# Preparing the tokens of the first projection in blocks of 416 after the first one, with the sums of squares on VectorE, the copies of K on ScalarE and part of the first weights loaded by GpSimd

## The chip, the cores and the metric

The kernel runs on one core of a Trainium2 chip. Its engines are TensorE (PE in the profile), VectorE (DVE), ScalarE (ACT) and GpSimd (POOL); SyncE (SP) issues DMAs, and so do the queues of ScalarE and GpSimd. Each engine takes its instructions in one fixed order and waits on semaphores. The metric is the device time of one execution in microseconds; the number given for a kernel is the median of its runs.

## The reference

One layer of a streaming encoder, for 2048 prompt tokens and 32 sample tokens. The part that the change touches is the beginning:

```
shift_m, scale_m, ... = split(silu(c) @ w_ada + b_ada)        # per sequence: prompt, sample
h = rmsnorm(x, g_pre_mix) * (1.0 + scale_m) + shift_m         # x: (tokens, 1024)
z = h @ w_in                                                  # (1024, 5136), all mixers' inputs
```

where rmsnorm multiplies x by 1 / sqrt(mean of squares + 1e-6). From z come a banded attention, a gated linear attention, their merge and output projection, and then a gated MLP with a causal convolution. All of that follows unchanged.

## The kernel before

**Layout.** Tokens are columns: x is read as xT, 8 slices k of 128 channels by 2080 tokens (2048 prompt, then 32 sample). Matmuls work on pairs: a number is split into a rounded hi part and the remainder lo, and mm3 (L74) makes three matmuls per product, hi with hi (L78), hi with lo (L79), lo with hi (L80). The normed tokens h are kept as two tiles of hi and lo, hA for the first four blocks of NB = 416 tokens and hB for the fifth.

**The first stage.** Here the kernel computes the adaLN vectors, norms all tokens, and already projects them on 512 columns of w_in, Q and K of the gated linear attention, in a "wave" (L341): for each block of 416 tokens, for each k, for four chunks of 128 output columns, three matmuls, all into four PSUM tiles (tag px, six buffers). So a block takes 96 matmuls of 416 columns. A wave ends with four evacuations (t_evac, L202): Q by ScalarE with a factor (L230), K by VectorE (L233), each into a tile tx (two buffers) that is stored by a DMA of ScalarE's queue (L235).

**The norm by half blocks** of NH = 208 tokens, ten of them, numbered hb. prep_load (L263) loads two tiles of four k each (tag xk, six buffers). prep_stats (L270) squares them on ScalarE (L276, L279), two k at a time, and adds them up: on VectorE for hb 0 and 1, on GpSimd for the others (L280, L281). rstd_bcast (L140) splits the sum (sh on ScalarE, sl on VectorE), and its finish multiplies it by a matrix of ones on TensorE, so that the sum over channels stands in every partition (pst, L148 and L149, a PSUM tile of the same tag px); then ScalarE takes Ln and Exp (L154, L155) and VectorE corrects with three operations (L156 to L158): the reciprocal root. prep_apply (L290) then makes, for each k, x times scale times root on VectorE (L299), the hi part with the shift on ScalarE (L300) and the lo part on VectorE (L301). For hb 2 and odd k GpSimd does the scaling (L288, L297). The last half block has its 176 prompt and 32 sample tokens apart, since their scale and shift differ.

**The adaLN vectors** scale and shift come in four pieces each: ada_load (L305) brings 1 MB in two DMAs, ada (L314) multiplies with packed matmuls (L320), the result is turned by four small matmuls (L327), and mod_finish adds bias and gain. Piece j gives channels k = 2j and 2j + 1, so the norm of block 0 proceeds two k at a time as pieces arrive.

**The weights** of the wave, two of 256 columns, are loaded in four pieces of two k each (w_pieces, L180; L187 is the DMA on SP, two buffers wr for both weights) and split (L191 ScalarE, L192 VectorE).

**What sets the order.** TensorE's order is the order in which the code is written (a manual schedule). The other engines' and queues' orders come from a scheduler that simulates the kernel ahead of time and prefers, among what is ready, what is written earlier. Written by hand is thus where in TensorE's stream the ones matmul of a half block stands: for hb 4 and later after the first k of each half of a wave (L434 to L436). Block 0 (L353 to L418) is written out with the adaLN pieces, the weights' pieces and hb 2 and 3 between its k. The blocks 1 to 4 follow in a loop over half blocks (L422). Then come the other columns of w_in in tiles of tokens (L564), with the later adaLN vectors on the side.

Of the kernel before, what the change touches and what calls it, by code (L numbers as in the profile page):

```python
# [20 lines left out]
KD = 8  # L21
# [9 lines left out]
NB = 416  # L31
# [27 lines left out]
def encoder_step(ctx: ExitStack, tc: tile.TileContext, I, O):  # L59
# [30 lines left out]
    onef = consts.tile([128, 128], F32, name="onef")  # L90
    nc.vector.memset(onef, 1.0)
    ones = consts.tile([128, 128], F32R, name="ones")
    nc.vector.tensor_copy(ones, onef)
# [46 lines left out]
    def rstd_bcast(pl, pps, tag, s, n, w, bufs=1):  # L140
# [5 lines left out]
        def finish():  # L146
# [6 lines left out]
            r = pl.tile([128, w], F32, name="rstd", tag="rstd", bufs=bufs)  # L153
# [4 lines left out]
            nc.vector.scalar_tensor_tensor(r[:, :n], t[:, :n], 1.5, r0[:, :n], op0=OP.add, op1=OP.mult)  # L158
            return r[:, :n]
# [20 lines left out]
    def w_pieces(wp, c0, n, w, kp, wr=2):  # L180
# [4 lines left out]
        def piece(kk):  # L185
            raw = wp.tile([128, kp, w], F32, name="wr", tag="wr", bufs=wr)
            d = nc.sync.dma_start(raw[:, :, :n], dap(w_in, kk * 128 * WIN + c0, [[WIN, 128], [128 * WIN, kp], [1, n]]))  # L187
# [14 lines left out]
    def t_evac(stg, kind, c, b, p):  # L202
# [22 lines left out]
        if kind == "g":  # L225

            nc.scalar.activation(x, p, AF.Tanh, scale=0.5)
            dst = sgT
        elif kind == "Q":
            nc.scalar.activation(x, p, AF.Copy, scale=0.125)  # L230
            dst = qbT
        else:
            nc.vector.tensor_copy(x, p)  # L233
            dst = kbT
# [8 lines left out]
    with ExitStack() as st:  # L243
# [8 lines left out]
        scp = pp.tile([128, KD, 32], F32, name="scp")  # L252
# [7 lines left out]
        XK = {}  # L260
        POOL = {2: (1, 3, 5, 7)}

        def prep_load(hb, q_=nc.sync):  # L263
            XK[hb] = []
            for k in range(0, KD, 4):
                x = pp.tile([128, 4, NH], F32, name="xk", tag="xk", bufs=6)
                q_.dma_start(x, dap(I["xT"], k * 128 * T + NH * hb, [[T, 128], [128 * T, 4], [1, NH]]))
                XK[hb].append(x)

        def prep_stats(hb, add):  # L270

            sq = pp.tile([128, 2, NH], F32, name="sq", tag="sq", bufs=2)
            for k in range(0, KD, 2):
                x = XK[hb][k // 4][:, k % 4:k % 4 + 2]
# [3 lines left out]
                s2 = pp.tile([128, 2, NH], F32, name="sq2", tag="sq2")  # L278
                nc.scalar.activation(s2, x, AF.Square)  # L279
                add.tensor_add(sq, sq, s2)  # L280
            add.tensor_add(sq[:, 0], sq[:, 0], sq[:, 1])  # L281
            return lambda: rstd_bcast(pp, psx, "px", sq[:, 0], NH, NH, 2)

        def prep_scale(hb):
            for k in POOL.get(hb, ()):
                for a, e, s in parts(NH * hb, NH):
                    xs = XK[hb][k // 4][:, k % 4, a:e]
                    nc.gpsimd.tensor_scalar(xs, xs, mod[:, 1, k, s:s + 1], 1.0, op0=OP.mult, op1=OP.mult)  # L288

        def prep_apply(hb, r, ks_=range(KD)):  # L290
            for k in ks_:
                for a, e, s in parts(NH * hb, NH):
                    hi, lo = [h_at(x, k, NH * hb + a, e - a) for x in range(2)]
                    xs = XK[hb][k // 4][:, k % 4, a:e]
                    s1, s2 = mod[:, 1, k, s:s + 1], mod[:, 0, k, s:s + 1]
                    if k in POOL.get(hb, ()):
                        nc.gpsimd.tensor_mul(xs, xs, r[:, a:e])  # L297
                    else:
                        nc.vector.scalar_tensor_tensor(xs, xs, s1, r[:, a:e], op0=OP.mult, op1=OP.mult)  # L299
                    nc.scalar.activation(hi, xs, AF.Identity, bias=s2)  # L300
                    nc.vector.scalar_tensor_tensor(lo, xs, s2, f32(hi), op0=OP.add, op1=OP.subtract)  # L301

# [11 lines left out]
        def ada(j, v):  # L314
# [7 lines left out]
            r = pp.tile([128, 256], F32, name="mr", tag="mr")  # L322
# [12 lines left out]
        prep_load(0)  # L335
        prep_load(1)
        ada_load(0, 0)
        first = [("Q", 1536), ("K", 1792)]
        w0, steps = zip(*[w_pieces(wp, c0, 256, 272, 2, 2) for _, c0 in first])
# [13 lines left out]
        fin0 = prep_stats(0, nc.vector)()  # L353
# [25 lines left out]
        for s_ in steps:  # L379
            s_[2]()  # L380
# [1956 lines left out]
```

## Time and profile before

| | us |
|---|---|
| median of 3 runs | 3160.36 |
| lowest and highest run | 3156.84, 3162.19 |
| the profiled execution | 3162.02 |
| its span, from first to last instruction | 3160.3 |
| first wave matmul (block 0) | 27.21 |
| first matmul after the last wave (block 4) | 163.85 |

The profile shows one execution. A row of the groups names the line, engine, operation, the tile written and those read, the shape, the count, the busy time, the mean duration in ns, and then the idle time of the engine just ahead of such instructions with what ended it. A row of the waits names who waited for whom: us in total, times, the longest. A row of the stretches gives for each engine the busy time and number of instructions, then the TensorE clock granted (1.00 is full), the DMA engines' busy share and GB/s. In the order of time a row begins with the start and the time it took; x4 means four instructions in a row. Durations of one instruction include time in which the next has already begun.

### The profile page before, as it was taken

What the parts mean: (1) busy time and instruction counts of PE and PEld (TensorE: products, weight loads), DVE (VectorE), ACT (ScalarE), POOL (GpSimd) and SP (SyncE); (2) the same over time, 40 slices, a digit from 0 to 9 for tenths busy, and PEclk for the clock granted to TensorE, in tenths of its full rate; (3) what the DMA queues carried; (4) which work ended last, traced back from release to release, by engine and by line L of the source; (5) the groups of instructions that cost most, each with busy time, mean ns of one, the idle gap of its engine ahead of it and who ended that gap; (6) DMA issues with size and microseconds to landing.
All of it is one profiled execution on the core that took longest, in us unless ns stands there. A gap on an engine that the chain in (4) does not pass through costs nothing. (4 is left out here: it accounts for less than half of the span.)

```text
span 3160.3 us, 56426 instructions
## 1 busy us (share of the span) xinstructions
PE 3047.7 (96%) x19748; PEld 2947.7 (93%) x19748; DVE 2239.8 (71%) x4879; ACT 1648.8 (52%) x3792; POOL 269.4 (9%) x427
## 2 busy tenths in 40 slices
PE   6999999999999999999999999999999999999997
PEld 4899999998999999988999899999999999999997
DVE  6735617774555555566677799998888778897877
ACT  4522224443555555544454655567666556576755
POOL 2201201112111111120000000000000000000001
PEclk9999999999999999999999999999999999999998
DMA  7354435554433334575457686788897667888784
GB/s 220 91 156 125 139 98 142 137 137 128 130 109 111 107 100 117 169 230 184 140 175 227 211 256 210 223 256 225 249 265 217 189 189 230 263 250 284 242 267 146
DMA packets 598478, 580.12 MB, mean 184 GB/s; under 512 B 53201, under 2 KB 526530, under 8 KB 598194
## 3 DMA queue, kind: packets, MB, share of 16 engines
q1 hardware_dynamic: 553026, 527.86, 56.2%
q10 hardware_dynamic: 44432, 47.34, 4.7%
q8 instruction: 155, 2.54, 0.3%
q0 software_dynamic: 736, 1.33, 0.2%
q14 instruction: 129, 1.06, 0.1%
HBM read 388.71 MB, written 187.65 MB: 182 GB/s over the span
## 5 line engine op out<-in xcount | busy, mean ns | idle before, releaser
L1882 PE MATMUL ad<-hA,hB 128*128 128x350 f32 (+2 forms) x1734 | 301.7, 324 | 3.8 <-DVE hB L1824 2.4
L1882 PEld LDWEIGHTS ad<-hA,hB 128*128 128x128 f32 x1734 | 282.5, 189 | 5.5 <-DVE hB L1824 3.3
L78 PE MATMUL pm<-hA,wh 128*128 128x416 f32 x768 | 287.4, 374 | 0.0
L79 PE MATMUL pm<-hA,wh 128*128 128x416 f32 x768 | 269.3, 351 | 0.0
L80 PE MATMUL pm<-hA,wl 128*128 128x416 f32 x768 | 269.3, 351 | 0.0
L1824 DVE TENSOR_TENSOR hA<-raws,hA 128x512 fp32r<-128x512 f32 (+1 forms) x367 | 241.9, 668 | 13.0 <-ACT hA L1819 12.7
L1819 ACT ACTIVATE hA<-raws 128x512 fp32r<-128x512 f32 (+1 forms) x367 | 222.0, 617 | 29.9 <-DMA raws<-in_w_up_dram 11.1
L1882 PE MATMUL ad<-hA,hA 128*128 128x348 f32 (+2 forms) x1308 | 225.5, 323 | 2.5 <-ACT work L2008 1.8
L1882 PE MATMUL g<-hA,hB 128*128 128x348 f32 (+2 forms) x1248 | 217.1, 323 | 6.4 <-ACT work L2004 3.5
L1882 PEld LDWEIGHTS ad<-hA,hA 128*128 128x128 f32 x1308 | 211.8, 188 | 3.9 <-ACT work L2008 2.4
L1882 PEld LDWEIGHTS g<-hA,hB 128*128 128x128 f32 x1248 | 202.3, 188 | 9.1 <-ACT work L2004 4.7
L1882 PE MATMUL ad<-hA 128*128 128x350 f32 (+2 forms) x1173 | 205.1, 324 | 4.2 <-DVE hA L1734 4.1
L1882 PEld LDWEIGHTS ad<-hA 128*128 128x128 f32 x1173 | 191.7, 190 | 5.0 <-DVE hA L1734 4.4
L1824 DVE TENSOR_TENSOR hB<-raws,hB 128x512 fp32r<-128x512 f32 (+1 forms) x289 | 190.9, 668 | 6.5 <-ACT hB L1819 6.1
L1819 ACT ACTIVATE hB<-raws 128x512 fp32r<-128x512 f32 (+1 forms) x289 | 175.8, 617 | 25.3 <-DMA raws<-in_w_up_dram 11.8
L69 ACT ACTIVATE pth<-pp 128x256 fp32r<-128x256 f32 (+1 forms) x288 | 106.4, 373 | 139.2 <-PE pp L1027 135.9
L72 DVE TENSOR_TENSOR ptl<-pp,pth 128x256 fp32r<-128x256 f32 (+1 forms) x288 | 118.1, 414 | 85.2 <-ACT pth L69 82.4
L78 PE MATMUL pn<-wh,hA 128*128 128x256 f32 (+1 forms) x624 | 176.9, 283 | 0.0
L79 PE MATMUL pn<-wl,hA 128*128 128x256 f32 (+1 forms) x624 | 176.3, 283 | 0.0
L80 PE MATMUL pn<-wh,hA 128*128 128x256 f32 (+1 forms) x624 | 176.1, 282 | 0.0
L1991 ACT COPY g<-ad 128x348 f32<-128x348 f32 (+2 forms) x102 | 44.3, 434 | 244.1 <-PE ad L1882 156.4
L1882 PE MATMUL g<-hA,hA 128*128 128x350 f32 (+2 forms) x894 | 157.4, 325 | 4.0 <-ACT g L1991 2.3
(507 smaller groups left out, 8468.6 us busy)
## 6 DMA issues: line engine op xcount, KB each, us to landing
raws<-in_w_up_dram SPq DMA_DIRECT2D x220, 256.0 KB, 4.3
raws<-sW SPq DMA_DIRECT2D x176, 256.0 KB, 3.8
sW<-raws SPq DMA_DIRECT2D x88, 256.0 KB, 3.6
raws<-in_w_down_dram SPq DMA_DIRECT2D x80, 256.0 KB, 5.2
wr<-in_w_in_dram SPq DMA_DIRECT2D x76, 256.0 KB, 3.2
sgT<-tx ACTq DMA_DIRECT2D x80, 208.0 KB, 1.9
wa<-in_w_ada_dram SPq DMA_DIRECT2D x64, 256.0 KB, 3.0
keys<-ks SPq DMA_DIRECT2D x128, 128.0 KB, 2.9
```

Source lines behind the costliest of these rows:

```text
L69: i = nc.scalar.activation(hi, src, AF.Copy)
L72: nc.vector.tensor_sub(lo, src, f32(hi))
L78: nc.tensor.matmul(out, ah, bh, start=first and i == 0, stop=False)
L79: nc.tensor.matmul(out, ah, bl, start=False, stop=False)
L80: nc.tensor.matmul(out, al, bh, start=False, stop=last and i == n - 1)
L1819: act = nc.scalar.activation(hi[:, :n], raw(i, n), AF.Copy)
L1824: nc.vector.tensor_sub(lo[:, :n], raw(i, n), f32(hi[:, :n]))
L1882: nc.tensor.matmul(out[:, :w], l_[:, k], r_[:, k, :w], start=first and k == 0 and i == 0, stop=k == n - 1 and i == 2, skip_group_check=True)
L1991: nc.scalar.copy(g[:, 0, :w], ad[:, 0, :w])
```

## The change

- After block 0 the norm goes by whole blocks of 416 tokens. Token tiles hold two k of a block (still six buffers); block 0 is loaded and normed in two halves as before.
- All sums of squares are VectorE's, of two k of 416 tokens at a time; GpSimd's sums and scalings go. The tiles sq, sq2, rstd have one buffer each, of the larger size.
- The ones matmul writes a PSUM tile of another pool (psm, tag pm) that is otherwise used later; px is left to the waves and the adaLN pieces.
- In blocks 1 to 3 the ones matmul of the next block stands behind six of the eight k of the wave, followed in the text by the next block's scaling and the load of the block after it. For block 1 it stands behind the sixth k of block 0.
- K is copied out of PSUM by ScalarE (t_evac's last branch).
- Of the two first weights the third and fourth piece (k from 4) are issued by GpSimd's queue (late=nc.gpsimd).
- Small tiles move: scp to another pool, mr into a tile of tag nx, the ones are made from ident in one operation.

```diff
     nc.vector.memset(eps, EPS)
-    onef = consts.tile([128, 128], F32, name="onef")
-    nc.vector.memset(onef, 1.0)
     ones = consts.tile([128, 128], F32R, name="ones")
-    nc.vector.tensor_copy(ones, onef)
+    nc.vector.tensor_scalar(ones, ident, 0.0, 1.0, op0=OP.mult, op1=OP.add)
+    onef = f32(ones)
...
-    def rstd_bcast(pl, pps, tag, s, n, w, bufs=1):
+    def rstd_bcast(pl, pps, tag, s, n, w, r=None):
...
             t = pl.tile([128, w], F32, name="rstt", tag="sl")
-            r = pl.tile([128, w], F32, name="rstd", tag="rstd", bufs=bufs)
             nc.scalar.activation(r0[:, :n], p[:, :n], AF.Ln, bias=eps, scale=1.0 / D)
...
             nc.vector.scalar_tensor_tensor(t[:, :n], t[:, :n], -0.5 / D, r0[:, :n], op0=OP.mult, op1=OP.mult)
-            nc.vector.scalar_tensor_tensor(r[:, :n], t[:, :n], 1.5, r0[:, :n], op0=OP.add, op1=OP.mult)
-            return r[:, :n]
+            nc.vector.scalar_tensor_tensor(r, t[:, :n], 1.5, r0[:, :n], op0=OP.add, op1=OP.mult)
+            return r
...
-    def w_pieces(wp, c0, n, w, kp, wr=2):
+    def w_pieces(wp, c0, n, w, kp, wr=2, late=nc.sync):
...
             raw = wp.tile([128, kp, w], F32, name="wr", tag="wr", bufs=wr)
-            d = nc.sync.dma_start(raw[:, :, :n], dap(w_in, kk * 128 * WIN + c0, [[WIN, 128], [128 * WIN, kp], [1, n]]))
+            d = (nc.sync if kk < KD // 2 else late).dma_start(raw[:, :, :n], dap(w_in, kk * 128 * WIN + c0, [[WIN, 128], [128 * WIN, kp], [1, n]]))
             if behind.pop():
...
         else:
-            nc.vector.tensor_copy(x, p)
+            nc.scalar.copy(x, p)
             dst = kbT
...
-        scp = pp.tile([128, KD, 32], F32, name="scp")
+        scp = pa.tile([128, KD, 32], F32, name="scp")
         nc.vector.memset(scp, 0.0)
...
-        XK = {}
-        POOL = {2: (1, 3, 5, 7)}
-        def prep_load(hb, q_=nc.sync):
-            XK[hb] = []
-            for k in range(0, KD, 4):
-                x = pp.tile([128, 4, NH], F32, name="xk", tag="xk", bufs=6)
-                q_.dma_start(x, dap(I["xT"], k * 128 * T + NH * hb, [[T, 128], [128 * T, 4], [1, NH]]))
-                XK[hb].append(x)
-        def prep_stats(hb, add):
-            sq = pp.tile([128, 2, NH], F32, name="sq", tag="sq", bufs=2)
+        XK, RT = {}, {}
+        def prep_load(b, ks_=range(0, KD, 2), a=0, n=NB):
+            for k in ks_:
+                if (b, k) not in XK:
+                    XK[b, k] = pp.tile([128, 2, NB], F32, name="xk", tag="xk", bufs=6)
+                nc.sync.dma_start(XK[b, k][:, :, a:a + n],
+                                  dap(I["xT"], k * 128 * T + NB * b + a, [[T, 128], [128 * T, 2], [1, n]]))
+        def prep_stats(b, a=0, n=NB):
+            sq = pp.tile([128, 2, NB], F32, name="sq", tag="sq")[:, :, :n]
             for k in range(0, KD, 2):
-                x = XK[hb][k // 4][:, k % 4:k % 4 + 2]
+                x = XK[b, k][:, :, a:a + n]
                 if k == 0:
...
                     continue
-                s2 = pp.tile([128, 2, NH], F32, name="sq2", tag="sq2")
+                s2 = pp.tile([128, 2, NB], F32, name="sq2", tag="sq2")[:, :, :n]
                 nc.scalar.activation(s2, x, AF.Square)
-                add.tensor_add(sq, sq, s2)
-            add.tensor_add(sq[:, 0], sq[:, 0], sq[:, 1])
-            return lambda: rstd_bcast(pp, psx, "px", sq[:, 0], NH, NH, 2)
-        def prep_scale(hb):
-            for k in POOL.get(hb, ()):
-                for a, e, s in parts(NH * hb, NH):
-                    xs = XK[hb][k // 4][:, k % 4, a:e]
-                    nc.gpsimd.tensor_scalar(xs, xs, mod[:, 1, k, s:s + 1], 1.0, op0=OP.mult, op1=OP.mult)
-        def prep_apply(hb, r, ks_=range(KD)):
+                nc.vector.tensor_add(sq, sq, s2)
+            nc.vector.tensor_add(sq[:, 0], sq[:, 0], sq[:, 1])
+            if a == 0:
+                RT[b] = pp.tile([128, NB], F32, name="rstd", tag="rstd")
+            return rstd_bcast(pp, psm, "pm", sq[:, 0], n, NB, RT[b][:, a:a + n])
+        def prep_apply(b, r, ks_=range(KD), a=0, n=NB):
             for k in ks_:
-                for a, e, s in parts(NH * hb, NH):
-                    hi, lo = [h_at(x, k, NH * hb + a, e - a) for x in range(2)]
-                    xs = XK[hb][k // 4][:, k % 4, a:e]
+                for c, e, s in parts(NB * b + a, n):
+                    hi, lo = [h_at(x, k, NB * b + a + c, e - c) for x in range(2)]
+                    xs = XK[b, k - k % 2][:, k % 2, a + c:a + e]
                     s1, s2 = mod[:, 1, k, s:s + 1], mod[:, 0, k, s:s + 1]
-                    if k in POOL.get(hb, ()):
-                        nc.gpsimd.tensor_mul(xs, xs, r[:, a:e])
-                    else:
-                        nc.vector.scalar_tensor_tensor(xs, xs, s1, r[:, a:e], op0=OP.mult, op1=OP.mult)
+                    nc.vector.scalar_tensor_tensor(xs, xs, s1, r[:, c:e], op0=OP.mult, op1=OP.mult)
                     nc.scalar.activation(hi, xs, AF.Identity, bias=s2)
                     nc.vector.scalar_tensor_tensor(lo, xs, s2, f32(hi), op0=OP.add, op1=OP.subtract)
+        def apply0(ks_):
+            prep_apply(0, r0, ks_, 0, NH)
+            prep_apply(0, r1, ks_, NH, NH)
...
                                  start=k < 4, stop=k >= 4)
-            r = pp.tile([128, 256], F32, name="mr", tag="mr")
+            r = stg.tile([128, 272], F32, name="mr", tag="nx")[:, :256]
             nc.vector.tensor_copy(r, p[:, :256])
...
         ada_load(0, 1)
-        prep_load(0)
-        prep_load(1)
+        prep_load(0, a=0, n=NH)
+        prep_load(0, a=NH, n=NH)
         ada_load(0, 0)
         first = [("Q", 1536), ("K", 1792)]
-        w0, steps = zip(*[w_pieces(wp, c0, 256, 272, 2, 2) for _, c0 in first])
+        w0, steps = zip(*[w_pieces(wp, c0, 256, 272, 2, 2, nc.gpsimd) for _, c0 in first])
...
-        fin0 = prep_stats(0, nc.vector)()
+        fin0 = prep_stats(0, 0, NH)
         ada_load(1, 1)
...
         r0 = fin0()
-        fin1 = prep_stats(1, nc.vector)()
+        fin1 = prep_stats(0, NH, NH)
         m1 = ada(0, 0)
...
         ps = wave_tiles()
-        fins = {}
         for s_ in steps:
...
         ada_load(2, 1)
-        prep_load(2)
         m0 = ada(1, 1)
...
         ada_load(3, 1)
-        prep_load(3)
-        prep_apply(0, r0, [0, 1])
-        prep_apply(1, r1, [0, 1])
+        apply0([0, 1])
         for s_ in steps:
             s_[2]()
+        prep_load(1, (0, 2))
         ada_load(3, 0)
-        fins[2] = prep_stats(2, nc.gpsimd)
         wave(0, (0, ), ps)
...
         m0 = ada(2, 1)
-        prep_apply(0, r0, [2, 3])
-        prep_apply(1, r1, [2, 3])
-        prep_load(4)
+        apply0([2, 3])
         for s_ in steps:
             s_[3]()
+        prep_load(1, (4, 6))
         wave(0, (1, ), ps)
...
         m1 = ada(2, 0)
-        fins[3] = prep_stats(3, nc.gpsimd)
+        fin = prep_stats(1)
         wave(0, (2, ), ps)
...
         m0 = ada(3, 1)
-        prep_apply(0, r0, [4, 5])
-        prep_apply(1, r1, [4, 5])
+        apply0([4, 5])
         wave(0, (3, ), ps)
         m0()
-        prep_scale(2)
         m1 = ada(3, 0)
-        r2 = fins.pop(2)()()
         wave(0, (4, ), ps)
         m1()
-        prep_apply(0, r0, [6, 7])
-        prep_apply(1, r1, [6, 7])
-        prep_apply(2, r2)
-        prep_load(5)
+        apply0([6, 7])
         wave(0, (5, ), ps)
-        f3 = fins.pop(3)()
-        wave(0, (6, ), ps)
-        r3 = f3()
-        wave(0, (7, ), ps)
-        prep_apply(3, r3)
-        fins[4] = prep_stats(4, nc.gpsimd)
+        r = fin()
+        prep_apply(1, r)
+        prep_load(2)
+        wave(0, (6, 7), ps)
         wave_evac(0, ps)
...
         hB.extend(arena2.tile([128, KD, NB], F32R, name=f"hB{x}") for x in range(2))
-        for s_ in range(2, 10):
-            b = s_ // 2
-            if s_ + 4 < 10:
-                prep_load(s_ + 4)
-            if s_ + 3 < 10:
-                fins[s_ + 3] = prep_stats(s_ + 3, nc.gpsimd)
-            k0 = 4 * (s_ % 2)
-            if s_ + 2 < 10:
-                fin = fins.pop(s_ + 2)()
-            if s_ % 2 == 0:
-                ps = wave_tiles()
-            if b < 4:
-                wave(b, range(k0, k0 + 1), ps)
-                prep_apply(s_ + 2, fin())
-                wave(b, range(k0 + 1, k0 + 4), ps)
-            elif s_ % 2 == 0:
-                wave(b, range(KD), ps, (0, 1))
-                wn = load_w(wp, 2048, 256, 272, 2, 2)
-            else:
-                wave(b, range(KD), ps, (2, 3))
-            if s_ % 2:
-                wave_evac(b, ps)
+        for b in range(1, 4):
+            ps = wave_tiles()
+            fin = prep_stats(b + 1)
+            wave(b, range(6), ps)
+            prep_apply(b + 1, fin())
+            if b < 3:
+                prep_load(b + 2)
+            wave(b, (6, 7), ps)
+            wave_evac(b, ps)
+        ps = wave_tiles()
+        wave(4, range(KD), ps, (0, 1))
+        wn = load_w(wp, 2048, 256, 272, 2, 2)
+        wave(4, range(KD), ps, (2, 3))
+        wave_evac(4, ps)
         prep.close()
```

## The prediction

> **What bounds the kernel now.** I read the page first, then the busy time by stretches, then who waited for whom inside the stretches that stand out, and last the order of time at one block boundary.
>
> ```profile
> span 3160.3 us, 56426 instructions
> PE 3047.7 (96%) x19748; PEld 2947.7 (93%) x19748; DVE 2239.8 (71%) x4879; ACT 1648.8 (52%) x3792; POOL 269.4 (9%) x427
> ```
>
> TensorE is busy for 96% of the span: 112.6 us in all is idle. The change lies in the stage up to the first projection's end, 164 us of 3160. So the question is how much of TensorE's idle time and slow clock lies there, and how much of that the change can reach. Whatever TensorE gains there is carried to the end, since all that follows is bound by it. Five token blocks of 416 columns go through the wave of Q and K; the stretches below are the start and then block 0, 1, 2, 3 and 4, cut where TensorE starts each of them.
>
> ```profile
> core 0: us, PE busy (x) PEld busy (x) DVE busy (x) ACT busy (x) POOL busy (x), PEclk, DMA share, GB/s
> 0.00:27.21 27.21, 12.63 (x81) 6.07 (x81) 13.10 (x40) 11.75 (x24) 0.70 (x6) 1.00 0.85 258
> 27.21:71.25 44.04, 33.29 (x186) 27.09 (x186) 31.05 (x67) 20.24 (x47) 17.31 (x20) 0.88 0.70 214
> 71.25:97.36 26.11, 22.71 (x101) 21.15 (x101) 20.61 (x46) 14.75 (x36) 13.29 (x11) 0.80 0.31 90
> 97.36:121.72 24.36, 20.00 (x102) 18.07 (x101) 18.50 (x43) 13.19 (x33) 8.01 (x9) 1.00 0.37 108
> 121.72:145.75 24.03, 21.22 (x102) 19.72 (x101) 19.16 (x57) 11.93 (x32) 2.16 (x4) 0.93 0.12 37
> 145.75:163.85 18.10, 18.10 (x97) 17.96 (x97) 13.63 (x36) 6.03 (x15) 0.00 (x0) 1.00 0.63 205
> ```
>
> Block 4, which has no later block to prepare, takes 18.10 us: 96 matmuls with nothing between them, 0.188 us each. Blocks 1, 2 and 3 do the same matmuls in 26.11, 24.36 and 24.03 us, together 74.50, though VectorE, ScalarE and GpSimd are far from full. So a chain of waits sets their length. 74.50 - 3 x 18.10 = 20.2 us is the most that the waits and the slow clock of these three can give back.
>
> ```profile
> PE px L78 <- ACT tx L230: 4.1, 4, 1.6
> PE pst L149 <- DVE sl L72: 2.3, 2, 1.7
> PE px L78 <- ACT hA L300: 2.1, 1, 2.1
> PE px L79 <- DVE hA L301: 2.1, 3, 0.8
> PE pst L148 <- ACT sh L69: 2.0, 1, 2.0
> ```
>
> These are TensorE's waits in blocks 1 to 3: for the copy out of a PSUM tile (4.1 us), for the normed tokens (hA, 4.2) and for the sum of squares (4.3), 12.6 us. The boundary from block 1 to 2, TensorE and then ScalarE:
>
> ```profile
> 97.36 0.42 PE L78 MATMUL px<-hA,wh 128*128 128x416 f32 x1
> 102.42 0.46 PE L78 MATMUL px<-hA,wh 128*128 128x416 f32 x1 [1.61 <-ACT tx L230]
> 103.32 0.37 PE L148 MATMUL pst<-sh,ones 128*128 128x208 f32 x1
> ...
> 100.78 1.18 ACT L300 ACTIVATE hA<-xk,mod 128x208 fp32r<-128x208 f32 x3 [0.86 <-DVE xk L299]
> 101.87 0.49 ACT L230 ACTIVATE tx<-px 128x416 f32<-128x416 f32 x1
> ```
>
> Twelve matmuls of the first k take 5.96 us (97.36 to 103.32) in place of 2.25. The second copy of Q stands in ScalarE's order behind the hi parts of the half block in preparation, and its PSUM tile is needed by the fourth chunk.
>
> **The sums and the size of the pieces.** Prices of the operations, one row each:
>
> ```profile
> L299 DVE SCALAR_TENSOR_TENSOR xk<-xk,mod,rstd 128x208 f32<-128x208 f32 x68 | 35.0, 558 | 0.4
> L280 POOL TENSOR_TENSOR sq<-sq,sq 128x416 f32<-128x416 f32 x24 | 29.9, 1246 | 40.0 <-ACT sq L279 39.8
> L301 DVE SCALAR_TENSOR_TENSOR hA<-xk,mod,hA 128x208 fp32r<-128x208 f32 x64 | 28.8, 497 | 1.9 <-ACT hA L300 1.9
> L279 ACT ACTIVATE sq<-xk 128x416 f32<-128x416 f32 x30 | 16.3, 544 | 17.4 <-POOL sq L280 11.9 <-DMA xk<-in_xT_dram 3.8 <-DVE sq L280 1.7
> L233 DVE COPY tx<-px 128x416 f32<-128x416 f32 x10 | 5.8, 584 | 6.5 <-DMA qbT<-tx 3.9 <-ACT rst L154 2.0 <-DMA wa<-in_w_ada_dram 0.6
> L230 ACT ACTIVATE tx<-px 128x416 f32<-128x416 f32 x10 | 4.9, 501 | 5.2 <-PE px L80 5.2
> L280 DVE TENSOR_TENSOR sq<-sq,sq 128x416 f32<-128x416 f32 x6 | 3.6, 593 | 4.5 <-ACT sq L279 4.5
> L299 DVE SCALAR_TENSOR_TENSOR xk<-xk,mod,rstd 128x176 f32<-128x176 f32 x8 | 3.2, 397 | 0.0
> L299 DVE SCALAR_TENSOR_TENSOR xk<-xk,mod,rstd 128x32 f32<-128x32 f32 x8 | 2.0, 246 | 0.0
> ...
> 73.40 1.46 DVE L299 SCALAR_TENSOR_TENSOR xk<-xk,mod,rstd 128x208 f32<-128x208 f32 x4
> ```
>
> The forms of 176 and 32 columns give VectorE's slope, (397 - 246) / 144 = 1.05 ns a column. One of 208 columns alone is then 0.397 + 32 x 1.05 ns = 0.43 us. Four undisturbed ones take 1.46 us: (1.46 - 0.43) / 3 = 0.343 us from one to the next. An operation of 416 columns then comes every 0.343 + 208 x 1.05 ns = 0.56 us. The means of 558 and 497 ns for the same 208 columns show what GpSimd's additions beside them cost: over the 64 to 68 operations, (558 + 497 - 2 x 430) x 66 = 13 us of VectorE.
>
> VectorE for one block, without disturbance. Before: 32 operations x 0.343 = 11.0, two chains of three for the reciprocal root at 0.43 each 2.6, two splits 0.7, two K copies 1.2, together 15.5. After: 16 x 0.56 = 9.0, one chain 3 x 0.65 = 2.0, one split 0.6, and new the sums of squares: three of 832 columns (593 ns + 416 x 1.05 = 1.03) and one of 416, 3.7; the K copies gone: 15.3. So VectorE takes over GpSimd's sums for nothing, since half the operations of the rest disappear, and GpSimd's disturbance goes. 15.3 fits under TensorE's 18.1. Block 4 has its last 32 columns by themselves, as before, and its preparation costs 2 us more, under the same cover.
>
> ScalarE per block: four squares of 832 columns at most 1.09 (twice 544), eight hi parts of 416 at about 0.55 (between the copy's 501 and the square's 544 ns), Ln, Exp and the split the same, 1.6, four copies 2.0 of which two (K) are new, four DMA issues 1.5: some 14 us of 18 (the issues by an estimate from SP's 0.37). It has room, so the K copies cost nothing themselves. But they add a wait in its queue, taken up below.
>
> **The chain across a boundary, after.** The matmul with the ones now stands behind six of the eight k of a block (T). In the trace it and the first scaling of the next tokens stand thus:
>
> ```profile
> 138.78 0.26 PE L148 MATMUL pst<-sh,ones 128*128 128x208 f32 x1
> ...
> 141.36 1.04 DVE L299 SCALAR_TENSOR_TENSOR xk<-xk,mod,rstd 128x176 f32<-128x176 f32 x4
> ```
>
> 2.58 us for 208 columns; with 416, the two matmuls grow by 0.1 each (0.188 us for 416 above), Ln and Exp by some 0.17 each (an estimate beneath VectorE's slope), three VectorE operations by 0.22 each: T + 3.8. VectorE in this trace does up to four scalings in a row (73.40 above); if they stand ahead of the first lo part, the first lo is ready at T + 3.8 + 4 x 0.56 + 0.65 = T + 6.7. TensorE has the two ones matmuls (0.4) and 24 matmuls (4.5) to do, to T + 4.9. It waits 1.8 us, and I add 0.2 for the copies: 2.0 per boundary in place of 5.96 - 2.25 = 3.7. From there TensorE takes 2.25 us per k and VectorE gives one every 1.12, so it doesn't wait again.
>
> Then the next T. The second half of the next tokens can be loaded only when the first half of this block's buffers is read out (six buffers of two k, four per block), at about T + 9. A load takes this long:
>
> ```profile
> 88.16 0.37 SPq L267 DMA_DIRECT2D xk<-in_xT_dram  x1
> ...
> 91.62 0.55 ACT L276 ACTIVATE sq<-xk 128x416 f32<-128x416 f32 x1 [1.58 <-DMA xk<-in_xT_dram]
> ...
> qbT<-tx ACTq DMA_DIRECT2D x10, 208.0 KB, 2.7
> ks<-ql POOLq DMA_DIRECT2D x10, 104.0 KB, 2.7
> ```
>
> 3.5 us from issue to use. T + 12.5; two squares and two sums in turn (the buffer for squares is single) 4.2, the last sum 0.6, the split 1.2: T + 18.5. TensorE reaches the next ones matmul at T + 4.9 + 2.0 + 13.5 = T + 20.4. 1.9 us of slack; I charge 0.5 for orders that don't fit. The block: 18.1 + 0.4 + 2.0 + 0.5 = 21.0, three of them 63.0 for 74.5: **-11.5 us**. Beneath, with no wait at all, 18.5; above, see the rivals.
>
> The clock: block 1 has 0.80 and 22.71 us of PE for what takes 20.00 in block 2, 2.7 us, with waits of 2.1 and 2.0 us in it; block 2 kept 1.00 with waits of 1.6 and 1.7. New waits of 2.0 lie between, nearer to the first by size but shorter in sum; I take 0 and keep 2.7 per block for the range. The Trainium skill's "TensorE: Matmul & The Clock Gate" (Part 1) puts the loss of clock at an idle window of about 3.4 us; by that the waits forecast here cost only themselves, and block 1 of this trace, whose waits are all shorter, speaks against taking it as a bound.
>
> **Block 0.** It keeps its half blocks, its adaLN pieces and its order. What changes: GpSimd's sums and scalings beside it go (17.31 us of its time here), the sums of block 1 come to VectorE (3.6), four VectorE scalings that GpSimd did come back in the larger form, and the third and fourth quarter of both weights are issued by GpSimd.
>
> ```profile
> L192 DVE TENSOR_TENSOR wl<-wr,wh 128x512 fp32r<-128x512 f32 x24 | 17.3, 723 | 19.0 <-ACT wh L191 18.7
> ...
> 50.20 1.55 DVE L192 TENSOR_TENSOR wl<-wr,wh 128x512 fp32r<-128x512 f32 x1
> 51.78 6.39 SPq L187 DMA_DIRECT2D wr<-in_w_in_dram  x4
> 55.58 0.63 ACT L191 ACTIVATE wh<-wr 128x512 fp32r<-128x512 f32 x1 [5.22 <-DMA wr<-in_w_in_dram]
> 59.82 0.53 PE L78 MATMUL px<-hA,wh 128*128 128x416 f32 x1 [2.97 <-ACT hA L300]
> ```
>
> SP's fourth quarter leaves at 51.78, right when VectorE has split the piece before in the same buffer (50.20 + 1.55). ScalarE stands 5.22 us for it, and TensorE 2.97 us for what is queued behind that. The wait is for the buffer, not for the queue, so another queue doesn't remove it; it frees SP, where the tokens stand behind. What can shorten it is that this split ran 1.55 us where the mean is 0.72, beside GpSimd, and that ScalarE's squares stood 11.9 us for GpSimd's sums (the row of the squares above), in part ahead of the weights. TensorE's idle time in this block is 44.04 - 33.29 = 10.8 us. Between nothing and 8 of it (the rest is the adaLN weights' own arrival, an estimate) I take **-3**, nearer the lower end since the buffer still rules. GpSimd's own price to issue is bounded by its store above: 2.7 us to landing, like ScalarE's, so the queue costs 0 to some 1 us per piece.
>
> The Trainium skill's "SBUF — State Buffer" ("Two separate sides") says that DMAs issued by GpSimd stand still while VectorE runs certain copies, 620 ns becoming 3100; by an estimate from that page the last pair would be 2.5 us late and the time 2.5 us longer. No run here shows it at this place, and the splits here are not copies.
>
> The eight smaller token loads at the start, for four, cost SP at most four more issues of 0.37 us (the SP row above), 1.5; I take 0, since transfers and not issues fill the start (DMA share 0.85 in its stretch). The ones tile and the moved small tiles: 0. Block 4 and all behind it: 0.
>
> **Sum**: -11.5 - 3 = -14.5. The profiled execution took 3162.0 us (span 3160.3 and 1.7 around it), the median of the runs is 3160.4; -14.5 on the median is **3146**.
>
> **Rivals.**
> *The chain is longer than TensorE's work* (0.21). The K copies wait on ScalarE for the store of the Q copy whose buffer they reuse (two buffers; 2.7 us to landing, plus copy 0.5 and issue 0.3), with hi parts of the next block queued behind and VectorE's lo parts behind those. Then the buffers come free some 2.5 us later, and the ones matmul waits 3.0 and not 0.5: 23.5 per block, 70.5 for three, -4; block 0 -1: 3155. For it: VectorE already stood 3.9 us for that store, and the copies move the wait. Against: the slack of 1.9 us.
>
> *The Q copies come behind all eight hi parts* (0.13), the other side. In the trace the second one did, behind half parts. Whole ones end at about T + 3.8 + 13 x 0.56 + 0.6, the copy at T + 12.3, which is 7.4 us after the boundary; TensorE does two chunks (1.1) meanwhile and idles 6.3, then runs cold as in block 1, 2.7: 18.5 + 9.0 = 27.5, three 82.5, +8.0: 3168. It decides where the idle time passes 24.8 - 18.5 = 6.3 us a boundary; ScalarE has gaps between hi parts now, each 1.12 us apart, into which a copy fits, which speaks against.
>
> *All is covered* (0.14): blocks of 18.9, -17.8, and block 0 loses 8: 3135.
>
> That GpSimd isn't out of it is so far true as it issues four DMAs; priced above.
>
> **Numbers.** Forecast 0.52, rivals 0.21, 0.13, 0.14. 0.2% is 6.3 us, about what a measurement of this kernel tells from none: faster (under 3154) holds the forecast and the covered case, 0.66; same 0.21; slower 0.13. The range reaches from beyond the covered case, 3132, to 3165, which takes in the long chain and part of the slow case.
>
> **What would show it.** Right: blocks 1 to 3 of about 21 us; the wait of TensorE for ScalarE's tx under 1 us a block; scalings of 416 columns with a mean under 0.68 us; no GpSimd work in the stage; the first projection's end some 14 us earlier and everything behind unchanged. Wrong: TensorE's ones matmul waiting 2 us or more per block, tx copies behind the eighth hi part, block 0 longer than 44 us, or a PEclk below 0.9 in blocks 1 to 3.

## The result and the profile after

The changed kernel takes 3143.3 us (median of 6 runs, 3139.6 to 3145.6) where the kernel before took 3160.9 (median of 6): a ratio of 0.9945, 95% interval 0.9935 to 0.9955, 17.6 us less. The forecast was 14.5 less. The profiled execution took 3142.3 us, 19.8 less than that of before.

The first lines of the page of after:

```profile
span 3140.6 us, 56253 instructions
PE 3041.1 (97%) x19740; PEld 2943.4 (94%) x19740; DVE 2222.3 (71%) x4808; ACT 1644.8 (52%) x3742; POOL 233.4 (7%) x391
```

The stretches of after, cut as before at the first wave matmul of each block and at the end of block 4. The columns are those of the table in the prediction: length, then busy time and number of instructions of PE, PEld, DVE, ACT and POOL, then the clock granted, the DMA engines' busy share and GB/s.

```profile
0.00:26.50 26.50, 12.88 (x81) 5.72 (x81) 12.80 (x39) 11.87 (x23) 0.70 (x6) 1.00 0.82 256
26.50:63.22 36.72, 30.94 (x184) 25.24 (x184) 23.11 (x57) 16.16 (x31) 3.12 (x4) 0.91 0.74 239
63.22:83.25 20.03, 18.88 (x98) 18.22 (x98) 16.06 (x26) 11.65 (x20) 0.00 (x0) 1.00 0.40 124
83.25:102.72 19.47, 18.91 (x98) 18.25 (x98) 15.05 (x25) 11.55 (x20) 0.00 (x0) 1.00 0.44 131
102.72:122.36 19.64, 18.90 (x98) 18.25 (x98) 14.25 (x26) 10.13 (x19) 0.00 (x0) 1.00 0.28 91
122.36:142.88 20.52, 19.02 (x97) 17.91 (x97) 14.94 (x42) 10.42 (x24) 0.57 (x2) 1.00 0.47 140
```

Blocks 1 to 3 went from 74.50 to 59.14 us (-15.4), block 0 from 44.04 to 36.72 (-7.3), the start from 27.21 to 26.50 (-0.7; it varies from 25.09 to 26.58 in the runs of the changed kernel and its variants below), and block 4 from 18.10 up to 20.52 (+2.4). The stage ends at 142.88 in place of 163.85: -21.0. Of the span -19.7 is left; the 2997 us behind the stage differ by +1.3 between the two executions.

TensorE's waits in blocks 1 to 3, and then in block 4 (who waited for whom, us in total, times, the longest):

```profile
PE px L79 <- DVE hA L291: 2.2, 3, 1.1
PE px L78 <- ACT hA L290: 0.3, 1, 0.3
...
PE px L79 <- DVE hB L291: 1.5, 3, 0.8
PE px L78 <- ACT hB L290: 0.2, 1, 0.2
```

The waits for a copy (tx) and for the sum of squares are gone, 4.1 and 4.3 us of the 12.6 before; what is left is the wait for the first normed tokens of a block, 2.5 us in three blocks where it was 4.2. The operations, by form (count, busy us, mean ns):

```profile
L289 DVE SCALAR_TENSOR_TENSOR xk<-xk,mod,rstd 128x416 f32<-128x416 f32 x24 | 14.3, 646 | 0.1
L291 DVE SCALAR_TENSOR_TENSOR hA<-xk,mod,hA 128x416 fp32r<-128x416 f32 x24 | 14.2, 644 | 0.0
L277 DVE TENSOR_TENSOR sq<-sq,sq 128x832 f32<-128x832 f32 x12 | 12.3, 1023 | 5.4 <-ACT sq L276 3.4 <-ACT sq L273 1.9
```

And one boundary, block 2 to 3, in TensorE's, VectorE's and ScalarE's order of time, ahead of which the ones matmul (L147) starts:

```profile
97.66 0.35 PE L147 MATMUL pst<-sh,ones 128*128 128x416 f32 x1
102.72 0.45 PE L78 MATMUL px<-hA,wh 128*128 128x416 f32 x1
103.73 0.46 PE L79 MATMUL px<-hA,wh 128*128 128x416 f32 x1 [0.56 <-DVE hA L291]
...
101.34 1.78 DVE L289 SCALAR_TENSOR_TENSOR xk<-xk,mod,rstd 128x416 f32<-128x416 f32 x3
103.04 1.77 DVE L291 SCALAR_TENSOR_TENSOR hA<-xk,mod,hA 128x416 fp32r<-128x416 f32 x3
...
114.48 0.59 DVE L72 TENSOR_TENSOR sl<-sq,sh 128x416 fp32r<-128x416 f32 x1 [0.62 <-ACT sh L69]
...
101.05 0.52 ACT L228 ACTIVATE tx<-px 128x416 f32<-128x416 f32 x1 [1.63 <-PE px L80]
102.03 1.77 ACT L290 ACTIVATE hA<-xk,mod 128x416 fp32r<-128x416 f32 x3 [0.45 <-DVE xk L289]
103.70 0.50 ACT L228 ACTIVATE tx<-px 128x416 f32<-128x416 f32 x1
```

From the ones matmul T = 97.66 the scalings begin at T + 3.7, three of them in a row, and the first lo part ends at about T + 6.0 (103.04 + 0.65); TensorE reaches the boundary at T + 5.1 and waits 0.56 us. Both copies of Q stand ahead of the fourth hi part. The next sum is split at T + 17.4 (114.48 + 0.59), the next ones matmul is reached at about T + 19.5.

### The profile page after: what moved, and what is told of

Its sections match the earlier page's. It is cut to its first block, busy times and chain, and to the rows that moved or that the text cites. A ratio compares the mean times of both kernels' runs of the same rounds, so it can differ in the third digit from the quotient of the medians.

```text
span 3140.6 us, 56253 instructions
## 1 busy us (share of the span) xinstructions
PE 3041.1 (97%) x19740; PEld 2943.4 (94%) x19740; DVE 2222.3 (71%) x4808; ACT 1644.8 (52%) x3742; POOL 233.4 (7%) x391
```

## The experiments

Three theories were set against each other. **G**: GpSimd's work beside VectorE was the cost, by disturbing VectorE and by its slow sums. **W**: the whole blocks are the gain, with one root chain per block, half as many operations, and one place for the ones matmul. **S**: the side edits are, that is the K copies, the PSUM tile of the ones matmul and the queue of the late weights.

Run times of one kernel lie some us apart and the chips differ by a few us, so each ratio is to the kernel before on the same chip. The stage itself repeats better: the table gives its parts from each run's trace, in us, and the wave from block 0's first matmul to block 4's end.

| kernel | ratio, 95% interval | blk 0 | 1 | 2 | 3 | 4 | wave |
|---|---|---|---|---|---|---|---|
| before | 1 | 44.04 | 26.11 | 24.36 | 24.03 | 18.10 | 136.6 |
| changed | 0.9945, 0.9935 to 0.9955 | 36.72 | 20.03 | 19.47 | 19.64 | 20.52 | 116.4 |
| changed, again | 0.9947, 0.9935 to 0.9960 | 38.44 | 19.17 | 19.46 | 19.65 | 20.51 | 117.2 |
| half blocks, GpSimd out | 0.9976, 0.9967 to 0.9985 | 40.45 | 24.57 | 22.60 | 20.57 | 18.11 | 126.3 |
| half blocks, all else changed | 0.9963, 0.9950 to 0.9975 | 42.04 | 23.54 | 23.65 | 18.45 | 18.11 | 125.8 |
| changed, sums on GpSimd | 0.9970, 0.9959 to 0.9982 | 41.53 | 20.44 | 20.63 | 20.65 | 20.50 | 123.8 |
| changed, scaling in halves | 0.9965, 0.9952 to 0.9979 | 36.87 | 23.87 | 21.04 | 20.67 | 21.94 | 124.4 |
| changed, K on VectorE | 0.9947, 0.9933 to 0.9960 | 37.54 | 21.07 | 20.09 | 19.92 | 20.43 | 119.0 |
| changed, weights on SP | 0.9931, 0.9918 to 0.9943 | 37.98 | 19.17 | 19.47 | 19.62 | 20.51 | 116.8 |
| changed, ones matmul in px | 0.9937, 0.9925 to 0.9950 | 36.94 | 20.05 | 19.47 | 19.63 | 20.50 | 116.6 |
| changed, GpSimd reading | 1.0004, 0.9996 to 1.0013 | 43.43 | 26.83 | 25.28 | 22.35 | 20.51 | 138.4 |
| changed, GpSimd writing | 0.9943, 0.9931 to 0.9956 | 36.82 | 20.06 | 19.47 | 19.64 | 20.51 | 116.5 |
| changed, ones earlier | 0.9941, 0.9927 to 0.9954 | 37.74 | 20.05 | 19.69 | 19.77 | 18.62 | 115.9 |

The changed kernel run twice gives a wave of 116.4 and 117.2 us, so differences of a us or less say nothing there. In the second run the first matmul behind block 4 comes at 143.57 us, a little later than the 142 to 143 that I expected of it.

**Half blocks, GpSimd out.** The kernel before with all sums and scalings on VectorE (the four calls of prep_stats after hb 1 alike):

```diff
-        POOL = {2: (1, 3, 5, 7)}
+        POOL = {}
-                fins[s_ + 3] = prep_stats(s_ + 3, nc.gpsimd)
+                fins[s_ + 3] = prep_stats(s_ + 3, nc.vector)
```

> The kernel before with one part of the change: all sums of squares and all scalings on VectorE, still by half blocks, all else as before. Three theories of the 17.6 us. G, GpSimd's disturbance of VectorE and its slow sums made blocks 1 to 3 long: at least half of the gain is here, 3151 us or less, scalings of 208 columns at 0.43 us mean and blocks of at most 22 us. W, the whole blocks (one root chain per block, half the operations, one place of the ones matmul) did it: VectorE has 15.5 + 4.3 = 19.8 us per block, over TensorE's 18.1, blocks stay at 23 to 24, 3157 to 3162. S, the side edits (K copies, the PSUM tile of the ones matmul, the queue of the weights): no change, 3159 to 3162.

Measured: 3156.1 us, ratio 0.9976, 0.24% less where the change has 0.55%. The wave is 10.3 us shorter, half of the change's 20.3. Its blocks 1, 2 and 3:

```profile
67.99:92.56 24.57, 23.22 (x101) 21.67 (x102) 22.40 (x62) 15.62 (x39) 0.00 (x0) 0.79 0.33 88
92.56:115.16 22.60, 20.27 (x102) 19.72 (x100) 17.90 (x49) 13.38 (x32) 0.00 (x0) 0.92 0.40 116
115.16:135.73 20.57, 18.97 (x102) 18.40 (x101) 17.67 (x56) 10.51 (x28) 0.00 (x0) 1.00 0.15 43
```

In the three blocks together, the scalings, and the largest row of TensorE's waits:

```profile
L299 DVE SCALAR_TENSOR_TENSOR xk<-xk,mod,rstd 128x208 f32<-128x208 f32 x46 | 17.6, 429 | 0.1
...
PE pst L148 <- DVE tx L233: 3.7, 3, 2.3
```

So neither G nor W alone. The scalings are at the 0.43 us that G gave, and GpSimd's part is there: 0.24 of 0.55%, somewhat less than the half that G asked for, and half of the wave's gain. But blocks 1 and 2 stay above 22 us, with VectorE busy for 22.4 and 17.9 of it, and block 1 has a clock of 0.79. The ones matmul now waits for K copies on VectorE.

**Half blocks, all else changed.** The same, and with the K copies on ScalarE, the ones matmul in psm, the late weights on GpSimd's queue:

```diff
-            return lambda: rstd_bcast(pp, psx, "px", sq[:, 0], NH, NH, 2)
+            return lambda: rstd_bcast(pp, psm, "pm", sq[:, 0], NH, NH, 2)
-            nc.vector.tensor_copy(x, p)
+            nc.scalar.copy(x, p)
-        w0, steps = zip(*[w_pieces(wp, c0, 256, 272, 2, 2) for _, c0 in first])
+        w0, steps = zip(*[w_pieces(wp, c0, 256, 272, 2, 2, nc.gpsimd) for _, c0 in first])
```

> The kernel before with everything of the change except the whole blocks: sums and scalings on VectorE, K copies on ScalarE, the ones matmul in the other PSUM pool, late weights on GpSimd's queue, but half blocks of 208 and the old places of the ones matmul. W: it keeps blocks 1 to 3 above 22 us, and only block 0 gains; 3152 to 3158. S: most of the gain, 3143 to 3148, more than the kernel with GpSimd out alone by 5 us or more. G: the same as with GpSimd out alone, within 2 us.

Measured: 3152.4 us, ratio 0.9963, wave 125.8. The side edits add 0.5 us to the wave's gain, within what it repeats to; in the time they add 3.7 us, with intervals that overlap. The 5 us or more that S asked for are not there, and G's 2 us can't be told from these runs. The ones matmul's wait for K copies is gone, but waits for the sums stand in its place:

```profile
PE pst L149 <- DVE sl L72: 3.3, 1, 3.3
PE pst L148 <- ACT sh L69: 2.2, 1, 2.2
```

What the whole blocks bring beyond everything else is 125.8 - 116.4 = 9.4 us of the wave: 13.0 in blocks 0 to 2, of which 3.6 go back in blocks 3 and 4, where half blocks take 18.45 and 18.11 us, shorter than whole ones.

**The changed kernel, sums on GpSimd:**

```diff
-                nc.vector.tensor_add(sq, sq, s2)
+                (nc.gpsimd if b else nc.vector).tensor_add(sq, sq, s2)
-            nc.vector.tensor_add(sq[:, 0], sq[:, 0], sq[:, 1])
+            (nc.gpsimd if b else nc.vector).tensor_add(sq[:, 0], sq[:, 0], sq[:, 1])
```

> The changed kernel with the sums of squares of blocks 1 to 4 given back to GpSimd, all else as changed. G: VectorE's operations beside the sums become slower (416 columns from 0.65 to some 0.85 us), the sums of 832 columns take some 2.4 us each in place of 1.0, the ones matmul waits: blocks 1 to 3 at 22 us or more, 3151 to 3158. W: blocks stay under 21 us and the loss is under 4 us, 3143 to 3147.

Measured: 3153.3 us, ratio 0.9970; the time is the one that G gave, but the blocks are not: 20.4 to 20.7 us, 0.9 more on average, as W had it. The larger part is in block 0, 41.53 for 36.72. The groups between 60 and 130 us:

```profile
L277 POOL TENSOR_TENSOR sq<-sq,sq 128x832 f32<-128x832 f32 x9 | 18.8, 2086 | 41.2 <-ACT sq L276 41.2
L291 DVE SCALAR_TENSOR_TENSOR hA<-xk,mod,hA 128x416 fp32r<-128x416 f32 x24 | 17.9, 797 | 2.4 <-ACT hA L290 2.4
L289 DVE SCALAR_TENSOR_TENSOR xk<-xk,mod,rstd 128x416 f32<-128x416 f32 x24 | 16.0, 716 | 0.1
```

The same operations of 416 columns take 797 and 716 ns in place of 644 and 646, and one sum 2.09 us on GpSimd where VectorE needs 1.02. In blocks 1 to 3 there is room for most of that. In block 0 the ones matmul for block 1 waits 3.4 us for its sum, where it waits 0.4 and 1.4 us in the two runs of the changed kernel, but also 2.5 us in the run with the weights on SP; the rest of block 0's loss was not followed up.

**The changed kernel, scaling in halves.** Each of the two VectorE and the one ScalarE operation of prep_apply in two of 208 columns:

```diff
-                for c, e, s in parts(NB * b + a, n):
+                for c, e, s in cuts(b, a, n):
+        def cuts(b, a, n):
+            return [(h + c, h + e, s) for h in range(0, n, NH) for c, e, s in parts(NB * b + a + h, NH)]
```

> The changed kernel with the scaling, hi and lo parts of blocks 1 to 4 in two operations of 208 columns for each k (twice as many operations), the sums, the root and the places as changed. If the halved number of operations carries the gain of the whole blocks: VectorE per block 15.3 + 16 x 0.13 = 17.4 us, ScalarE some 16, both near TensorE's 18.5, so waits come back, 2 us per block or more, 3149 or more. If the place of the ones matmul and the single root chain carry it: under 0.7 us per block, 3143 to 3146.

Measured: 3151.1 us, ratio 0.9965, the wave 8.0 us longer. TensorE's waits in blocks 1 to 3:

```profile
PE pst L147 <- ACT sh L69: 3.5, 3, 2.1
PE px L78 <- ACT hA L293: 1.6, 3, 0.6
PE pst L148 <- DVE sl L72: 0.5, 3, 0.2
```

The wait for the next sum of squares is back. In block 1 it is 2.1 us in one piece, and the clock falls to 0.93; TensorE is busy there for 21.03 us with what takes 18.9 at a clock of 1.00:

```profile
61.96:85.83 23.87, 21.03 (x98) 19.60 (x98) 18.58 (x44) 13.68 (x29) 0.00 (x0) 0.93 0.38 117
```

So the halved number of operations is not a detail: it is what leaves VectorE and ScalarE the time in which the next sums are made. With it undone, blocks 1 to 3 take 65.6 us, as much as with half blocks (65.6) and 6.4 more than with whole ones (59.1), though the root chain and the place of the ones matmul are the changed ones. Block 0 is another matter: it stays at 36.87 us, where half blocks take 42.04, so what the whole blocks bring there does not come from the number of operations.

**The changed kernel, K on VectorE** (the diff's line of t_evac undone):

> The changed kernel with the K copies back on VectorE. S: VectorE waits for the store behind the tx buffer and the boundary grows, 2 us or more per block, 3149 or more. W and G: VectorE has 1.2 us per block to spare, 3142 to 3146.

Measured: 3149.3 us where the kernel before took 3164.7 on that chip, ratio 0.9947, the wave 1.8 to 2.7 us longer than in the two runs of the changed kernel, 0.3 to 1.9 us in each of blocks 1 to 3. A small cost, of a size that no theory named; in the time it can't be told from nothing.

**The changed kernel, weights on SP** (nc.gpsimd left out of the call of w_pieces):

> The changed kernel with the late weights' loads back on SP. If the other queue carries block 0's gain of 7.3 us: block 0 back at 42 us or more, 3148 to 3151. If it is the sums that left GpSimd (as the prediction has it, which took the buffer and not the queue as the limit): block 0 within 1.5 us of the changed 36.7, 3142 to 3145.

Measured: 3144.3 us, ratio 0.9931, wave 116.8, block 0 in 37.98 us. The queue of the late weights brings nothing that these runs show.

**The changed kernel, ones matmul in px** (psx, "px" in place of psm, "pm"):

> The changed kernel with the ones matmul's result back in the PSUM tiles px that the waves use. S: the next wave waits for tiles, 1 to 4 us per block, 3146 to 3155. W and G: four of six buffers are the wave's, two are free for it as before, no change, 3142 to 3145.

Measured: 3145.5 us, ratio 0.9937, wave 116.6. Nothing, as W and G had it. K on VectorE and px together, which is where the ones matmul waited for K copies with half blocks, were not tried with whole blocks.

**GpSimd reading, and GpSimd writing.** 80 subtractions on a tile of GpSimd's own, started by the last split of the weights; in the second kernel the loop is range(240) and its line nc.gpsimd.memset(dose, 0.0):

```diff
+        dose = stg.tile([128, 272], F32, name="dose", tag="ns", bufs=1)
+        nc.gpsimd.memset(dose[:, 256:], 0.0)
+        nc.gpsimd.tensor_copy(dose[:, :256], f32(w0[1][1][:, 7, :256]))
+        for i in range(80):
+            nc.gpsimd.tensor_sub(dose, dose, dose)
```

> The changed kernel with 80 subtractions of 272 columns on GpSimd, on a tile of its own that nobody waits for, started when the last weights are split (about 48 us): the disturbance by itself, some 55 to 80 us of GpSimd beside VectorE in blocks 0 to 3, two to three times what the kernel before had there. G: scalings and lo parts of 416 columns from 0.65 to 0.85 us or more, VectorE per block past 18 us, blocks of 20.5 us or more, 3147 to 3158. W: VectorE slows but has room of 3 us per block; under 3 us in all, 3142 to 3146.

> The changed kernel with 240 memsets of 272 columns on GpSimd in place of the 80 subtractions: a GpSimd as busy, which writes SBUF and reads nothing. If GpSimd's reads of SBUF are what holds VectorE's operations of two SBUF inputs (the Trainium skill, SBUF - State Buffer, Who interferes with whom, says so): scalings of 416 columns stay at 0.65 us and the time at the changed kernel's, within 3 us. If any use of SBUF by GpSimd does: 0.75 us or more, and 5 us or more lost.

Measured: 3165.9 us, ratio 1.0004, with the subtractions: the whole gain is gone, and more than G had said. With the memsets 3145.3 us, 0.9943: nothing is lost. The groups between 40 and 165 us of the one and then of the other:

```profile
L388 POOL TENSOR_TENSOR dose<-dose 128x272 f32<-128x272 f32 x80 | 69.1, 864 | 6.3
L289 DVE SCALAR_TENSOR_TENSOR xk<-xk,mod,rstd 128x416 f32<-128x416 f32 x24 | 21.2, 930 | 0.1
L291 DVE SCALAR_TENSOR_TENSOR hA<-xk,mod,hA 128x416 fp32r<-128x416 f32 x24 | 20.7, 912 | 0.0
```

```profile
L388 POOL MEMSET dose<- 128x272 f32 x240 | 78.5, 327 | 13.8
L289 DVE SCALAR_TENSOR_TENSOR xk<-xk,mod,rstd 128x416 f32<-128x416 f32 x24 | 14.3, 649 | 0.1
L291 DVE SCALAR_TENSOR_TENSOR hA<-xk,mod,hA 128x416 fp32r<-128x416 f32 x24 | 14.3, 648 | 0.0
```

GpSimd is busy 69 us in the one and 79 in the other. VectorE's scalings take 930 ns in the mean of the run with operations that read SBUF, and 649 beside those that only write it; undisturbed they take 646. Five of the 24 ran after the subtractions had ended at 122.5 us, and took 641. Once it is started, no semaphore joins GpSimd's work to VectorE's here. Two steps of the root, between 48 and 122 us of the run with the subtractions:

```profile
L156 DVE SCALAR_TENSOR_TENSOR rstd<-rstt,rst 128x416 f32<-128x416 f32 x3 | 2.7, 910 | 0.1
L154 DVE SCALAR_TENSOR_TENSOR rstt<-pst,rst 128x416 f32<-128x416 f32 x3 | 1.8, 592 | 1.4 <-ACT rst L153 1.3
```

Both take 592 to 593 ns in the changed kernel. L156, with two inputs in SBUF, is slowed, and L154, which reads one of its two from PSUM, is not. So it is operations of two SBUF inputs that GpSimd's reading slows, though not each one (L155 took 592, 592 and 989 ns). Subtractions and memsets differ in length too, 864 against 327 ns; that this plays no part was not shown. The Trainium skill states the rule in "SBUF — State Buffer", "Who interferes with whom"; this pair of runs agrees with it, 930 against 649 ns.

**The changed kernel, ones earlier.** The ones matmul of blocks 3 and 4 behind five k:

```diff
-            wave(b, range(6), ps)
+            n1 = 5 if b > 1 else 6
+            wave(b, range(n1), ps)
-            wave(b, (6, 7), ps)
+            wave(b, range(n1, 8), ps)
```

> The changed kernel with the ones matmul of blocks 3 and 4 behind five k of the wave before in place of six, 2.25 us earlier, all else as changed. If the waits at the boundaries and block 4's 20.5 us come from the chain that starts at the ones matmul: block 4 at 18.6 to 19.2, block 3's start without its 0.6 us wait, at the price of a wait of 0.1 to 0.8 us for the split; 1.5 to 2.5 us in the trace, about 3141. If they come from VectorE's 16 more small operations whatever the start: block 4 stays at 20 us or more, 3143.

Measured: block 4 in 18.62 us in place of 20.51, and the ones matmuls wait 0.7 + 0.2 us in their turn. The wave is 115.9 us, too near to 116.4 to tell; the time, 3145.5 us and 0.9941 beside 3147.5 and 0.9947 of the changed kernel on the same chip, has the forecast direction but is not told from it by these runs. Block 4's longer stretch is thus the start of its chain: with five k there is time for the 16 more operations of its last 32 tokens.

## Why the prediction was right, point by point

**What bounds it: right.** The stage's waits were the place, and what TensorE gained there reached the end of the span but for 1.3 us, which is less than the runs of one kernel differ.

**VectorE's sums: right.** 0.65 us for 416 columns was forecast and 0.646 measured; 1.03 for a sum of 832 and 1.023 measured; VectorE has 14 to 16 us of work per block where 15.3 was said. That it takes over GpSimd's sums "for nothing" holds: it is busy for 45.4 us in blocks 1 to 3, where it was 58.3. The four scalings that I called undisturbed ran beside one of GpSimd's sums, and there it was the sum that took longer, 3.24 us where the mean is 1.25:

```profile
73.58 3.24 POOL L280 TENSOR_TENSOR sq<-sq,sq 128x416 f32<-128x416 f32 x1 [2.41 <-ACT sq L279]
```

The price read from them held all the same: three scalings of 416 columns come 0.57 us apart where 0.56 was forecast. ScalarE's hi parts take 0.64 us and not 0.55, at no cost, since it is busy for 10 to 12 us of a block.

**The chain across a boundary: right in its steps, too dear in its size.** T + 3.8 was T + 3.7. I had four scalings ahead of the first lo part, and three stood there: T + 6.0 in place of T + 6.7. The charge of 2.0 + 0.5 us per block was 1.2: the mean block of 19.71 less 18.1 less 0.4. The next split at T + 18.5 was T + 17.4. Blocks 1 to 3 gave 15.4 us and not 11.5.

**The clock: right in the result, by waits shorter than forecast.** Blocks 1 to 4 show 1.00, with waits of up to 1.1 us. I had forecast waits of 2.0 and taken no loss of clock for them. The run with scaling in halves has one wait of 2.1 us in block 1, and lost 2.1 us to the clock there; the kernel with half blocks and GpSimd out has 0.79 in its block 1, 23.22 us of PE for work that takes 18.9. So with the waits as I had them, some 2 us per block could have come on top (an estimate from these two runs), which the range held and the sum did not.

**Block 0: the mis-sized term.** -3 was taken, the trace has -7.3, and -5.6 in the second run. I counted GpSimd's disturbance and missed that the norm of hb 2, scalings and all, stood inside block 0 and that the whole block's now starts at its end. VectorE was busy for 31.05 us in block 0 before, 30.5 with half blocks and GpSimd out, and is for 23.1 after. GpSimd out alone shortened block 0 by 3.6 us, which is about the term as it was argued; the rest needs the whole blocks. The number of operations isn't it, as the run with scaling in halves shows; that it is the place of the norm was not tried by itself.

I took the buffer and not the queue as what holds the weights, from the fourth quarter alone. For the third quarter it was SP's queue. VectorE had freed both buffers by 30.3 us, and SP issued the loads at 36.56, behind two loads of tokens (at 33.97); in the changed kernel with the weights on SP they go out at 30.00 (the third row):

```profile
29.65 0.69 DVE L192 TENSOR_TENSOR wl<-wr,wh 128x512 fp32r<-128x512 f32 x1 [0.75 <-ACT wh L191]
36.56 2.16 SPq L187 DMA_DIRECT2D wr<-in_w_in_dram  x2
...
30.00 2.12 SPq L185 DMA_DIRECT2D wr<-in_w_in_dram  x2
```

Earlier weights alone don't shorten the block, though: with half blocks and all else changed GpSimd issues the third quarter from 27.40 us on and the fourth from 36.24, and block 0 takes 42.04 us. How much of the block's remaining 36.7 us is the adaLN weights' arrival was not tried.

**Block 4: wrong.** "Under the same cover" was said of its 2 us more of preparation, and the cover was gone, since its chain starts 5.2 us before the boundary (the ones matmul at 117.16, the boundary at 122.36) and no longer in halves. It cost 2.4 us, and starting the chain one k earlier gives 1.9 of it back.

**The sum: nearer than its terms.** Blocks 1 to 3 gave 3.9 us more than forecast and block 0 gave 4.3 more; block 4 took back 2.4, which I had at 0, and the stretch behind it 1.3. By the traces that makes 19.7 with the start, by the medians 17.6. That the forecast of 14.5 came within 3.1 us is owed in part to errors that cancel.

**The rivals.** The long chain didn't come: the ones matmul of blocks 2 to 4 did not wait. Nor did the copies come behind the hi parts: ScalarE's order put both copies of Q ahead of the fourth, as the gaps between them suggested. The covered case is nearest on blocks 1 to 3 (56.7 forecast there, 59.1 measured) and on block 0, and was missed for block 4. The stall of DMAs issued by GpSimd, of which the Trainium skill's "SBUF — State Buffer" ("Two separate sides") warns, can't be read from GpSimd's own time: each of the four took 0.72 to 0.93 us, and ahead of the first three stood the wait for the buffer. From issue to landing they took 6.7 us in the median, where SP's four of the same size between 20 and 63 us took 3.7; whether the issuing queue or the traffic beside them makes that difference stays open. It cost nothing that shows: with all of them on SP, block 0 took 37.98 us where it took 36.72 and 38.44. The first two, and the two rows of issues:

```profile
29.02 0.93 POOL L185 DMA_DIRECT2D wr<-in_w_in_dram  x1 [27.65 <-DMA wr<-in_w_in_dram]
30.41 0.74 POOL L185 DMA_DIRECT2D wr<-in_w_in_dram  x1 [0.46 <-DVE wl L190]
...
wr<-in_w_in_dram SPq DMA_DIRECT2D x4, 256.0 KB, 3.7
wr<-in_w_in_dram POOLq DMA_DIRECT2D x4, 256.0 KB, 6.7
```

## What to carry to other kernels

Work on an idle engine is not free when it slows the engine that is short. Giving GpSimd's sums and scalings to VectorE, in half blocks, left VectorE busy for 88.5 us in blocks 0 to 3, where it had been 89.3 without them: its other work became faster by about what the new work cost. Where a preparation runs beside a full engine, count its operations, not only its elements: half as many for the same tokens left the time in which the next chain could start in blocks 1 to 3. And when a chain is moved later for the steady state, look at the last turn of the loop by itself; its piece was longer here and its cover was gone.

## What the runs showed of the hardware that was not expected

The size of the disturbance: 69 us of GpSimd subtractions that nobody waits for took the ratio from 0.9945 to 1.0004, some 18.7 us, and the wave from 116.4 or 117.2 to 138.4 us, while 79 us of GpSimd memsets cost nothing.
